# A hybrid decoder layer: the relative bias stored as 23 equal rows a head instead of 128

## The chip, the cores and the metric

The kernel runs on one core of one Trainium2 chip. The metric is the time of one execution on the device in microseconds; the engines are TensorE (PE, with its weight loads as PEld), VectorE (DVE), ScalarE (ACT), GpSimd (POOL) and SyncE (SP), and transfers run on 16 DMA engines.

## The reference

One decoder layer on 256 tokens of width 2048, all in float32: a joint input projection, a Conformer convolution branch and a differential attention branch side by side, an output projection, a cross-attention into 256 memory tokens, a gated FFN with a causal convolution, and a final norm. What matters here is the bias of the differential attention. Each of 8 heads has two score maps, and both get the same bias, which depends only on the distance of query and key:

```python
bias = bias_dist_t[:, jnp.clip(rel, 0, s - 1)].astype(jnp.float32)     # rel = q_pos - k_pos
logits = logits.reshape(b, H_DIFF, 2, Q_BLOCK, s) + bias[None, :, None]
logits = jnp.where(causal[None, None, None], logits, NEG_INF)
```

So within a head the bias matrix has equal diagonals: row q is row 0 shifted by q.

## The kernel before

**Weights.** All matmuls are float32 products made of two parts: a weight chunk of 128 x 1024 (512 KB) is loaded (`raw`), ScalarE rounds it to `hi` (line 157) and VectorE subtracts it to `lo` (line 158), and TensorE multiplies with both. SyncE issues the loads in order (line 146); `raw`, `hi` and `lo` have four buffers each, so a load waits for the subtraction four chunks back, and a rounding for TensorE four chunks back.

**Steps.** The kernel counts its weight chunks, and the other work of the phase is placed at such steps (`STEPS`, `PAIR`). Chunks 0 to 31 are the convolution's gates, 32 to 39 the values of heads 0 to 3, 40 to 71 the queries and keys of four pairs of heads, 8 chunks each. A chunk of a pair is twelve matmuls (lines 209 to 211). TensorE's order is written out by hand; the order on the other engines is made by the framework's planner from modelled times, with hints (`issue_after`) that hang the convolution's taps (line 342, VectorE) on a chunk's subtraction.

**Bias.** At step 43 `bias_rows` multiplies the table of 32 buckets with a one-hot matrix and gets, for each of 8 heads, one row of 384 values: column m is the bias of distance 255 - m, and columns of negative distance hold -1e30, which is the causal mask. ScalarE copies it to `brow` (8 partitions), and GpSimd writes it to a scratch tensor `scr` in memory (line 365). Head by head, `load_bias` reads it back to 128 partitions of 256 columns (line 370), also from GpSimd's queue, with two buffers.

**Heads.** A pair's queries and keys are turned (`turn`, lines 454 and 455, copied by ScalarE at line 457). `scores` multiplies them to logits (lines 466 and 469) in one buffer of PSUM, VectorE adds the bias (line 474), and the softmax and the combination of the two maps follow on VectorE and ScalarE (lines 477 to 485). The stages of a pair come between the next eight chunks: `turn` of its first head at 2 steps behind the pair's end, `scores` of the first and `turn` of the second at 3, `scores` of the second at 4, so for the first pair at steps 50, 51, 51 and 52.

Of the kernel before, what the change touches and what calls it, by code (L numbers as in the profile page):

```python
# [12 lines left out]
F32 = mybir.dt.float32  # L13
# [6 lines left out]
P = 128  # L20
S = 256
NMEM = 256
D = 2048
# [4 lines left out]
NH = 8  # L28
NB = 32
# [10 lines left out]
# columns of the packed per-partition parameters  # L40
# [9 lines left out]
# A step is the number of weight chunks before it: the gates' chunks are 0-31, the values of heads 0-3 take 32-39, the  # L50
# pairs of heads 40-71, the values of heads 4-7 72-79, the memory 80-95, the output projection 96-127, the queries 128-135.
# Behind its chunk, the tensor engine's other work comes at these steps.
# [5 lines left out]
# the same within a pair of heads, from the pair's end  # L58
PAIR = ((2, "turn", 0), (3, "scores", 0), (3, "turn", 1), (4, "scores", 1), (10, "combine", 1), (8, "combine", 0))
# operations of the queue behind each chunk, from that step on  # L60
# [7 lines left out]
def trunk_kernel(ctx, tc, xT_d, memT_d, mem_d, par_d, tab_d, hot_d, gf_d, wa_d, wck_d, wv_d, wqk_d,  # L68
# [19 lines left out]
    # ---- resident data  # L88
# [12 lines left out]
    # the tensor engine's clock rises while it is busy  # L101
# [6 lines left out]
    # ---- work of the other engines that is spread over the weight chunks: behind the rounding (ScalarE) or the  # L108
    # subtraction (VectorE) of a given chunk, and a queue behind the subtractions
# [18 lines left out]
    # ---- work of the tensor engine between the weight chunks, one stage after each  # L128
# [11 lines left out]
    # ---- weight chunks: raw -> (hi, lo), hi + lo == raw exactly  # L140
    sent = []

    def weight(src, name, dst=None, halved=False):
        raw = wp.tile([P, 1024], F32, tag="raw", bufs=4, name="raw_" + name)
        if not halved:
            sent.append(SP.dma_start(out=raw, in_=src).ins)
        hi, lo = dst or (wp.tile([P, 1024], F32R, tag=t, bufs=4, name=f"{t}_{name}") for t in ("hi", "lo"))
        if halved:
            # the first chunk, each half in front of its k-tile of x
            for k, w in enumerate((slice(0, 512), slice(512, 1024))):  # L150
                SP.dma_start(out=raw[:, w], in_=src[:, w])
                SP.dma_start(out=xT[:, k:k + 1, :], in_=xT_d[:, k:k + 1, :])
                A.copy(out=hi[:, w], in_=raw[:, w])
                V.tensor_tensor(out=lo[:, w], in0=raw[:, w], in1=hi[:, w].bitcast(F32), op=ALU.subtract)
            split_x(0)
            return hi, lo
        rounded = A.copy(out=hi, in_=raw)  # L157
        fill(rounded, V.tensor_tensor(out=lo, in0=raw, in1=hi.bitcast(F32), op=ALU.subtract))  # L158
        return hi, lo

    def quarter(name):
        """[hi | lo] of four k-tiles of an activation."""
        return act.tile([P, 4, 2 * S], F32R, tag="act", name=name)
# [4 lines left out]
    def split(dst, src, scale):  # L168
        """dst = [hi | lo] of src * scale (per partition)."""
        hi, lo = dst[:, 0:S], dst[:, S:2 * S]  # L170
        if scale is None:
            A.copy(out=hi, in_=src)
            V.tensor_tensor(out=lo, in0=src, in1=hi.bitcast(F32), op=ALU.subtract)
        else:
            A.activation(out=hi, in_=src, func=AF.Copy, scale=scale)
            V.scalar_tensor_tensor(out=lo, in0=src, scalar=scale, in1=hi.bitcast(F32), op0=ALU.mult,
                                   op1=ALU.subtract)

    def part_b(tiles, c, src, acts, name, first, last, narrow=False):
        """Four k-tiles of two n-tiles, weights stationary: tiles[n] = [w.T @ hi(act) | corrections];  # L180
        narrow: all in the first half."""
        hi, lo = weight(src, f"{name}_{c}")
        for kk in range(4):
            k = 4 * c + kk
            for n in range(2):
                o = kk * S + n * P
                begin, end = first and kk == 0, last and kk == 3
                if narrow:
                    T.matmul(tiles[n][:, 0:S], hi[:, o:o + P], acts(k)[:, 0:S], start=begin, stop=False)
                    T.matmul(tiles[n][:, 0:S], hi[:, o:o + P], acts(k)[:, S:], start=False, stop=False)  # L190
                else:
                    T.matmul(tiles[n], hi[:, o:o + P], acts(k), start=begin, stop=False)  # L192
                T.matmul(tiles[n][:, 0:S] if narrow else tiles[n][:, S:], lo[:, o:o + P], acts(k)[:, 0:S],  # L193
                         start=False, stop=end)
        stage()
# [5 lines left out]
    def part_a(tiles, c, src, acts, name, halved=False):  # L201
        """Two k-tiles: tiles[t] = (tokens of t) x 512 columns, activations stationary."""
        hi, lo = weight(src, f"{name}_{c}", halved=halved)
        for kk in range(2):
            k = 2 * c + kk
            w = slice(kk * 512, kk * 512 + 512)
            for t in range(2):
                ah, al = acts(k)[:, t * P:t * P + P], acts(k)[:, S + t * P:S + t * P + P]
                T.matmul(tiles[t], ah, hi[:, w], start=k == 0, stop=False)  # L209
                T.matmul(tiles[t], ah, lo[:, w], start=False, stop=False)  # L210
                T.matmul(tiles[t], al, hi[:, w], start=False, stop=k == KT - 1)  # L211
        stage()
# [7 lines left out]
    def sum_halves(out, pst, name):  # L220
        """out = main + corrections"""
# [4 lines left out]
    def rsqrt(out, ms, n, eps, shape, name):  # L226
        """out = 1 / sqrt(ms / n + eps), one Newton step behind the table's root."""
# [10 lines left out]
    def sum_all(acc, name):  # L238
        """Sums over the partitions of acc [P, S], on every partition."""
        m = sm_ps("ms_" + name)  # L240
        T.matmul(m[:, 0:S], ones, acc, start=True, stop=True)
        return m[:, 0:S]

    def sum_tok(parts, name):
        """out[p, t] = the sum of parts[:][:, t*128 + p] over their partitions."""
# [6 lines left out]
    def to_row(out, tok, name):  # L252
        """out[p, t*128 + c] = tok[c, t], on every partition p."""
# [8 lines left out]
    # ---- x: split, statistics  # L262
# [7 lines left out]
    def split_x(c):  # L270
        """Two k-tiles."""
# [5 lines left out]
    def total(t):  # L277
        """Sum over the tiles of t [P, 4, S], in place; its first tile is returned."""
# [25 lines left out]
    # ---- convolution module: gate and depthwise convolution  # L304
    gated = {}

    def gate(b):
        """Channel tiles 2b, 2b + 1: [second half | first half] of the projection, tokens on partitions."""
# [42 lines left out]
    # ---- relative bias and lambda  # L351
# [5 lines left out]
    # every row p of a head in memory alike; read back with a pitch shorter by one, row p is shifted by p  # L357
    scr = dr.tile([NH, P, BW], F32, name="scr")

    def bias_rows():  # L360
# [4 lines left out]
        G.dma_start(out=scr, in_=brow.unsqueeze(1).broadcast_to([NH, P, BW]))  # L365

    def load_bias(hd):
        bias = ph.tile([P, S], F32, tag="bias", bufs=2, name=f"bias{hd}")
        base = scr[hd, 0, P - 1:P - 1 + S]
        G.dma_start(out=bias, in_=bass.AP(tensor=base.tensor, offset=base.offset, ap=[[BW - 1, P], [1, S]]))  # L370
# [14 lines left out]
    # ---- differential attention: values  # L385
# [8 lines left out]
    # ---- convolution module: layer norm, silu (into the first half of mix)  # L394
# [39 lines left out]
    # ---- differential attention: heads  # L434
    o4, oss, s_last = {}, {}, [None]

    def pair(b):
        """Queries (scaled) and keys of two heads, tokens on partitions."""
# [20 lines left out]
    def scores(hd):  # L459
        """Both maps of a head, combined, but for the factor r1 of each query."""  # L460
# [10 lines left out]
        for qt in range(2):  # L471
# [10 lines left out]
            # p1 - lam p2, over r1: e1 + e2 * (-lam s1 / s2)  # L482
# [53 lines left out]
    def attend(b, qk):  # L536
        """The stages of a pair of heads, spread over the eight chunks of the next projection."""
# [7 lines left out]
    # ---- memory: split, statistics, keys  # L545
# [16 lines left out]
    def mem_square(t, c):  # L562
        """Sums of squares of a half of the tokens' rows."""
# [8 lines left out]
    def mem_queue(c):  # L572
        """The splits of two quarters, one to each of the next chunks."""
# [63 lines left out]
    # ---- output projection; residual in place; statistics  # L637
# [27 lines left out]
    # ---- cross attention  # L665
# [62 lines left out]
    # ---- its projection; where a part of it can go ahead, heads 0 and 1 first  # L728
# [44 lines left out]
    # ---- gated FFN  # L773
# [9 lines left out]
    def conv_f(i, u, out):  # L783
        """out = causal 3-tap convolution of channel tile i, whose projection u lacks the norm's factor."""
# [7 lines left out]
    for j in range(FT):  # L792
# [23 lines left out]
        if 4 <= j < 12:  # L816
            # residual to token-major
# [9 lines left out]
    # ---- down projection: eight banks, [token tile][column block]  # L827
# [38 lines left out]
    # ---- the last tiles bank after bank; final norm  # L866
# [4 lines left out]
    for t in range(2):  # L871
# [18 lines left out]
        # 1 / sqrt(v) = y0 * (1.5 - 0.5 v y0 y0)  # L890
# [21 lines left out]
# ---- host: layout only  # L912
# [9 lines left out]
def _one_hot():  # L922
    """Column m stands for the distance 255 - m; row NB marks what causality hides."""
# [8 lines left out]
def _cols(v):  # L932
    """(n*128,) -> (128, n)"""
# [3 lines left out]
def _feat(x):  # L937
    """(tokens, D) -> [p, k, token]"""
# [3 lines left out]
def _pair_chunks(w, first, second):  # L942
    """Blocks of two 128-column tiles of w (K, N): [block, chunk of 4 k-tiles, p, k, 256]."""
# [8 lines left out]
def _reorder(w, tiles):  # L952
    """The column tiles of w in that order."""
# [3 lines left out]
def _wide_chunks(w):  # L957
    """(K, n*512) -> [column block, chunk of 2 k-tiles, p, 1024]."""
# [57 lines left out]
```

## Time and profile before

| what | value |
|---|---|
| three runs, median | 1220.07 us (1219.28 to 1221.32) |
| profiled execution: span | 1219.7 us; the page gives no other time for it |
| TensorE busy | 1191.3 us (98%) |
| VectorE busy | 890.7 us (73%) |
| ScalarE busy | 683.2 us (56%) |
| GpSimd busy | 7.5 us (1%) |
| mean granted clock of TensorE | 0.989 |
| DMA | 227.62 MB, mean 187 GB/s |

The span is the time from the first to the last instruction on the core. Busy shares are means over all stages; an engine's wait counts only where something that sets the end is behind it. Times in the rows are microseconds from the span's start. A time to landing is the time from a DMA's issue until all its data have arrived.

### The profile page before, as it was taken

How to read it: one execution, taken by the hardware profiler on the slowest of the kernel's cores; microseconds unless marked ns; L12 is line 12 of the kernel's file. 1: busy time of each engine (PE TensorE's matmuls, PEld its weight loads, DVE VectorE, ACT ScalarE, POOL GpSimd, SP SyncE). 2: the span in 40 equal slices, each digit the busy share in tenths (PEclk: the TensorE clock that was granted, in tenths of full speed). 3: DMA queues.
4: the chain of work that ended last, by engine and by line, in shares of the span. 5: the costliest groups of instructions: out<-in, count | busy, mean ns of one | idle time of the engine just before them, and what ended most of it. 6: DMA issues, size and time to landing. Idle time of an engine off the chain costs nothing.

```text
span 1219.7 us, 16959 instructions
## 1 busy us (share of the span) xinstructions
PE 1191.3 (98%) x6186; PEld 1005.6 (82%) x6186; DVE 890.7 (73%) x1469; ACT 683.2 (56%) x1111; POOL 7.5 (1%) x19
## 2 busy tenths in 40 slices
PE   9999949999999999999999999999999999999997
PEld 7888738888888898888888888888888888888885
DVE  7899759998676778877777777777777756555554
ACT  8644336887755666755555555555555545444443
POOL 0000000000000000000000000000000000000000
PEclk9999979999999999999999999999999999999998
DMA  9656656566565636555665565555555467555541
GB/s 314 207 188 193 151 153 203 182 217 198 160 203 190 188 109 202 181 184 174 214 185 187 190 188 183 186 187 190 185 182 187 172 206 256 190 187 186 189 151 69
DMA packets 64164, 227.62 MB, mean 187 GB/s; under 512 B 7661, under 2 KB 7917, under 8 KB 63952
## 3 DMA queue, kind: packets, MB, share of 16 engines
q1 hardware_dynamic: 62784, 223.85, 56.5%
q0 software_dynamic: 1152, 2.68, 1.5%
q8 instruction: 48, 0.79, 0.2%
q14 instruction: 36, 0.29, 0.1%
q10 hardware_dynamic: 144, 0.01, 0.0%
HBM read 222.83 MB, written 3.67 MB: 186 GB/s over the span
## 4 chain that ended last, share of the span: by engine, by line
PE 93%; DMA 3%; DVE 2%; ACT 1%; issue 0%; SPq 0%; ACTq 0%
PE up L192 27%; PE up L193 14%; PE acc L840 5%; PE acc L841 5%; PE acc L842 5%; PE wo L192 5%; PE wo L193 2%; PE a L210 2%; PE a L211 2%; PE a L209 2%; DMA raw_qk<-in_wqk 2%; PE acc_lg L840 2%; PE acc_lg L841 2%; PE acc_lg L842 2%; PE qk L209 2%; PE qk L211 1%
## 5 line engine op out<-in xcount | busy, mean ns | idle before, releaser
L192 PE MATMUL up<-hf,hi_up 128*128 128x512 f32 x1408 | 497.8, 399 | 0.0
L193 PE MATMUL up<-hf,lo_up 128*128 128x256 f32 x1408 | 395.1, 281 | 0.0
L192 PEld LDWEIGHTS up<-hf,hi_up 128*128 128x128 f32 x1408 | 264.4, 188 | 64.8
L158 DVE TENSOR_TENSOR lo_up<-raw_up,hi_up 128x1024 fp32r<-128x1024 f32 x176 | 215.5, 1225 | 83.2 <-ACT hi_up L157 75.2
L157 ACT CAST hi_up<-raw_up 128x1024 fp32r<-128x1024 f32 x176 | 185.0, 1051 | 153.8 <-PE up L192 112.5
L193 PEld LDWEIGHTS up<-hf,lo_up 128*128 128x128 f32 x1408 | 265.9, 189 | 0.2
L158 DVE TENSOR_TENSOR lo_dn<-raw_dn,hi_dn 128x1024 fp32r<-128x1024 f32 x84 | 102.8, 1225 | 72.5 <-ACT hi_dn L157 72.3
L157 ACT CAST hi_dn<-raw_dn 128x1024 fp32r<-128x1024 f32 x84 | 88.1, 1049 | 64.7 <-PE acc_lg L842 54.0
L841 PE MATMUL acc<-lo_dn,gh 128*128 128x512 f32 x252 | 99.7, 396 | 0.0
L842 PE MATMUL acc<-hi_dn,gl 128*128 128x512 f32 x252 | 99.7, 395 | 0.0
L342 DVE SCALAR_TENSOR_TENSOR y<-ga,par,y 128x249 f32<-128x249 f32 (+17 forms) x240 | 99.0, 463 | 0.0
L840 PE MATMUL acc<-hi_dn,gh 128*128 128x512 f32 x252 | 98.7, 396 | 0.0
L192 PE MATMUL wo<-mix,hi_wo 128*128 128x512 f32 x256 | 89.3, 395 | 0.0
L193 PE MATMUL wo<-mix,lo_wo 128*128 128x256 f32 x256 | 70.6, 278 | 0.0
L223 ACT COPY corr_up<-up 128x256 f32<-128x256 f32 x88 | 32.9, 374 | 66.0 <-PE up L193 66.0
L157 ACT CAST hi_qk<-raw_qk 128x1024 fp32r<-128x1024 f32 x32 | 33.5, 1052 | 51.9 <-DMA raw_qk<-in_wqk 22.6
L224 DVE TENSOR_TENSOR u<-up,corr_up 128x256 f32<-128x256 f32 x88 | 37.1, 421 | 28.7 <-ACT corr_up L223 28.7
L209 PE MATMUL qk<-hi_qk,h 128*128 128x512 f32 x128 | 52.0, 406 | 5.3 <-ACT hi_qk L157 5.3
L840 PEld LDWEIGHTS acc<-hi_dn,gh 128*128 128x128 f32 x252 | 47.4, 188 | 11.5
L192 PEld LDWEIGHTS wo<-mix,hi_wo 128*128 128x128 f32 x256 | 47.9, 188 | 10.8
L842 PEld LDWEIGHTS acc<-hi_dn,gl 128*128 128x128 f32 x252 | 47.4, 188 | 11.4
L841 PEld LDWEIGHTS acc<-lo_dn,gh 128*128 128x128 f32 x252 | 47.4, 188 | 11.3
(300 smaller groups left out, 2007.1 us busy)
## 6 DMA issues: line engine op xcount, KB each, us to landing
raw_up<-in_wup SPq DMA_DIRECT2D x176, 512.0 KB, 3.5
raw_dn<-in_wdn SPq DMA_DIRECT2D x88, 512.0 KB, 4.5
raw_qk<-in_wqk SPq DMA_DIRECT2D x32, 512.0 KB, 4.0
raw_wo<-in_wo SPq DMA_DIRECT2D x32, 512.0 KB, 3.6
raw_a<-in_wa SPq DMA_DIRECT2D x31, 512.0 KB, 4.1
raw_v<-in_wv SPq DMA_DIRECT2D x16, 512.0 KB, 3.6
raw_ck<-in_wck SPq DMA_DIRECT2D x8, 512.0 KB, 3.8
raw_cv<-in_wck SPq DMA_DIRECT2D x8, 512.0 KB, 4.2
```

The costliest lines, as they stand in the source:

```text
L157: rounded = A.copy(out=hi, in_=raw)
L158: fill(rounded, V.tensor_tensor(out=lo, in0=raw, in1=hi.bitcast(F32), op=ALU.subtract))
L192: T.matmul(tiles[n], hi[:, o:o + P], acts(k), start=begin, stop=False)
L193: T.matmul(tiles[n][:, 0:S] if narrow else tiles[n][:, S:], lo[:, o:o + P], acts(k)[:, 0:S], start=False, stop=end)
L209: T.matmul(tiles[t], ah, hi[:, w], start=k == 0, stop=False)
L211: T.matmul(tiles[t], al, hi[:, w], start=False, stop=k == KT - 1)
L223: A.copy(out=c, in_=pst[:, S:])
L224: V.tensor_tensor(out=out, in0=pst[:, 0:S], in1=c, op=ALU.add)
L342: V.scalar_tensor_tensor(out=y[:, j, s:], in0=gated[j][:, 0:S - s], scalar=w, in1=y[:, j, s:], op0=ALU.mult, op1=ALU.add)
L840: T.matmul(acc[t][n], ah, hi, start=f == 0, stop=False)
L841: T.matmul(acc[t][n], ah, lo, start=False, stop=False)
L842: T.matmul(acc[t][n], al, hi, start=False, stop=f == FT - 1)
```

## The change

Two places change; elsewhere the diff only takes comments out. `scr` gets 23 rows of 384 values a head instead of 128, all alike as before. The read-back then goes through memory in two steps: partition p = 16a + b starts at a rows less 16a, and b rows less b, instead of p rows less p. Both ways partition p gets columns 127 - p to 382 - p. The largest row touched is 7 + 15 = 22.

```diff
-    # every row p of a head in memory alike; read back with a pitch shorter by one, row p is shifted by p
-    scr = dr.tile([NH, P, BW], F32, name="scr")
+
+    REP = P // 16 + 15
+    scr = dr.tile([NH, REP, BW], F32, name="scr")
 ...
-        G.dma_start(out=scr, in_=brow.unsqueeze(1).broadcast_to([NH, P, BW]))
+        G.dma_start(out=scr, in_=brow.unsqueeze(1).broadcast_to([NH, REP, BW]))
 ...
-        G.dma_start(out=bias, in_=bass.AP(tensor=base.tensor, offset=base.offset, ap=[[BW - 1, P], [1, S]]))
+        G.dma_start(out=bias, in_=bass.AP(tensor=base.tensor, offset=base.offset,
+                                          ap=[[BW - 16, P // 16], [BW - 1, 16], [1, S]]))
```

## Rows read from the trace of the kernel before

**Rows 1.** The page's 40 slices of the span, busy tenths.

```profile
PE   9999949999999999999999999999999999999997
```

**Rows 2.** Busy time by stretch; behind it clock, DMA share, GB/s.

```profile
122.00:152.20 30.20, 30.20 (x134) 24.16 (x132) 22.88 (x44) 10.03 (x13) 1.10 (x1) 1.00 0.63 152
152.20:178.60 26.40, 10.60 (x38) 7.33 (x37) 12.76 (x23) 7.08 (x8) 1.09 (x2) 0.68 0.62 156
178.60:265.00 86.40, 86.22 (x439) 69.44 (x440) 84.52 (x191) 68.35 (x166) 3.23 (x6) 1.00 0.60 199
...
150.00:155.00 5.00, 2.36 (x13) 1.76 (x11) 0.00 (x0) 0.00 (x0) 0.00 (x0) 0.96 0.50 85
```

**Rows 3.** The chain of waits, 139 to 180 us: start, length, what.

```profile
140.70 28.35 DMA raw_qk<-in_wqk
```

**Rows 4.** ScalarE in order of time, 144 to 175 us: start, length, instruction.

```profile
144.21 0.48 ACT L445 ACTIVATE qk<-qk,rx_tok 128x256 f32<-128x256 f32 x1
156.61 1.04 ACT L157 CAST hi_qk<-raw_qk 128x1024 fp32r<-128x1024 f32 x1 [11.92 <-DMA raw_qk<-in_wqk]
...
171.33 0.58 ACT L457 COPY qkT<-qkT 128x512 f32<-128x512 f32 x1
```

**Rows 5.** TensorE in order of time, from 149 to 180 us.

```profile
149.04 0.39 PE L209 MATMUL qk<-hi_qk,h 128*128 128x512 f32 x1
...
151.76 0.27 PE L454 MATMUL qkT<-ident,qk 128*128 128x128 f32 x1
...
152.09 0.27 PE L455 MATMUL qkT<-ident,qk 128*128 128x128 f32 x1
...
171.96 0.80 PE L466 MATMUL lg<-qkT 64*128 64x128 f32 x4 [9.06 <-ACT qkT L457]
...
178.61 0.49 PE L466 MATMUL lg<-qkT 64*128 64x128 f32 x4 [0.94 <-DVE L L474]
...
179.47 0.50 PE L209 MATMUL qk<-hi_qk,h 128*128 128x512 f32 x1
```

**Rows 6.** DMA issues (120 to 133, 133.6 to 135 us, whole span): KB each, us to landing.

```profile
raw_qk<-in_wqk SPq DMA_DIRECT2D x5, 512.0 KB, 3.6
...
raw_qk<-in_wqk SPq DMA_DIRECT2D x1, 512.0 KB, 21.6
...
xT<-in_xT SPq DMA_DIRECT2D x7, 256.0 KB, 6.6
...
scr<-brow POOLq DMA_DIRECT2D x1, 1536.0 KB, 35.5
bias<-scr POOLq DMA_DIRECT2D x8, 128.0 KB, 3.4
```

**Rows 7.** GpSimd in order of time, 0 to 300 us.

```profile
133.66 1.10 POOL L365 DMA_DIRECT2D scr<-brow  x1 [130.76 <-ACT brow L364]
169.40 1.09 POOL L370 DMA_DIRECT2D bias<-scr  x2 [34.64 <-DMA scr<-brow]
178.76 0.54 POOL L370 DMA_DIRECT2D bias<-scr  x1 [8.26 <-DVE L L474]
```

**Rows 8.** GpSimd's DMA queue, 135-140 and 150-155 us: packets, MB, share.

```profile
q0 software_dynamic: 405, 0.25, 50.8%
...
q0 software_dynamic: 52, 0.24, 40.7%
```

**Rows 9.** VectorE in order of time, 143 to 204 us.

```profile
157.69 1.23 DVE L158 TENSOR_TENSOR lo_qk<-raw_qk,hi_qk 128x1024 fp32r<-128x1024 f32 x1 [12.36 <-ACT hi_qk L157]
...
164.71 1.23 DVE L158 TENSOR_TENSOR lo_qk<-raw_qk,hi_qk 128x1024 fp32r<-128x1024 f32 x1 [5.02 <-ACT hi_qk L157]
...
170.22 1.23 DVE L158 TENSOR_TENSOR lo_qk<-raw_qk,hi_qk 128x1024 fp32r<-128x1024 f32 x1 [3.13 <-ACT hi_qk L157]
...
177.45 1.01 DVE L474 TENSOR_TENSOR L<-lg,bias 128x256 f32<-128x256 f32 x2
...
203.06 1.02 DVE L474 TENSOR_TENSOR L<-lg,bias 128x256 f32<-128x256 f32 x2
```

## The prediction

> **What bounds the kernel now.** I read the page's slices first. TensorE is busy nine tenths or more of every slice but one: the sixth, from 152 to 183 us, reads 4 [rows 1]. So the kernel is bound by TensorE, and a change outside it pays only in that hole. A table of three stretches cuts the hole out: from 122.0 to 152.2 us TensorE is busy throughout, from 152.2 to 178.6 it is busy 10.60 of 26.40 us at a clock of 0.68, and from 178.6 to 265, past the end of the pairs of heads, it is full again [rows 2]. The chain of waits says what the hole is: one piece of 28.35 us, a chunk of query and key weights on its way from memory, released at last at 169.05 [rows 3]; behind it the chain goes on over the rounding and VectorE's work, up to a bias add, to logits on TensorE.
>
> Then the queues. ScalarE rounds each weight chunk and stands idle for 11.92 us in front of the one at 156.61, for the weights' DMA, and again in front of the next; the copy of the turned queries (L457) stands behind those roundings in its queue, at 171.33, and TensorE's logits wait 9.06 us for it [rows 4, 5]. The weights were asked for early enough: a chunk takes 3.6 us to land between 120 and 133 us, the one issued at 134.97 takes 21.6 [rows 6], the one in the chain, issued at 140.70, 28.35. What is new at that moment is the write of the bias rows: GpSimd issues it at 133.66, it takes 35.5 us, and the first read-back starts at 169.40, when it has landed [rows 6, 7]. The software queue holds 51 to 41% of the sixteen engines' time meanwhile, and between 150 and 155 us the DMA share is 0.50 at 85 GB/s: by that I read eight engines full and eight empty, while the weights wait [rows 2, 8]. That is what is late: the half of every weight chunk that lies behind the write on those eight engines.
>
> **The change, part by part.** The write: 8 heads x 128 rows x 1536 B = 1.573 MB become 8 x 23 x 1536 B = 0.283 MB. The software queue moves 0.24 MB in 5 us [rows 8], so 0.048 MB a us; the old write is 32.8 us by that, and 2.7 of its 35.5 us lie around the moving. The new one is 0.283 / 0.048 + 2.7 = 8.6 us, and lands at 133.66 + 8.6 = 142.3. From below the nearest row is a read-back, 128 KB in 3.4 us; from above it is the old write itself, 35.5 us, if the time went by something other than bytes; an x load of 256 KB, nearly the new size, takes 6.6 us [rows 6]. I take 8.6, nearest to that last row.
>
> What is late then? The chunk issued at 134.97 (call it 51, by the kernel's own count of chunks) has its half on the eight engines behind the write. If none of that moves before 142.3 and half a chunk then takes half of 3.6 us, it lands at 144.1, the next two at 145.9 and 147.7. ScalarE wants the first at 144.69, after the four query and key copies [rows 4]; the following ones wait anyway for TensorE to free the rounded chunk four back, at 146.3, 149.0 and 151.8 (a chunk of 2.72 us apart, the last at the end of the matmuls before 151.76 [rows 5]). So no rounding is late.
>
> VectorE next, which has work without a gap in the old trace from 170 on: from the subtraction at 157.69 to the end of the bias add at 178.46 are 20.77 us, less its waits of 5.02 and 3.13, so 12.6 us of work [rows 9]. With the rounding of chunk 51 done at 145.7 it ends at 158.4.
>
> TensorE: between the end of the first turn (152.20) and the logits at 178.61 it does four things. Chunk 51: twelve matmuls, as from 149.04 to 151.76, 2.72 us. The logits of head 0: as from 178.61 to 179.47, 0.86. The turn of head 1: four transposes 0.11 apart from 151.76 on, 0.44, as the one that ended at 152.20. Chunk 52: 2.72. Together 6.74, since the engine no longer idles and its clock stays at 1.00 as in the stretch before [rows 2, 5]. The logits at 178.61 start at 152.20 + 6.74 = 158.94, with VectorE done 0.5 us earlier. The gain is 178.61 - 158.94 = 19.67 us: 15.80 us of idle time and 3.87 of slow matmuls.
>
> From there TensorE has no gap up to the end of the pairs in the old trace, so the whole is shifted and nothing later is given back: the stages behind run on the same prefetch, and the weights' queue is paced by VectorE's subtractions. The cover is thin in one place, VectorE's 0.5 us: each us by which chunk 51 lands after 145.2, that is the write takes over 9.8 us, costs TensorE up to one.
>
> The read-backs keep 128 rows of 1 KB and one issue of 0.54 us each; only the source's steps differ, eight blocks of 16 rows. They were 3.4 us. Bounds: 2.7 us by the write's rate (0.131 / 0.048), and 6.8 if they go on half the engines; I take 3.4 to 6.8 and cost it at nothing, because the bias of heads 0 and 1 is now issued from 142.3 for a use at 157.5, and the third, issued at 178.76, is used at 203.06, 24 us later [rows 7, 9]. Without that cover each would cost its own length. GpSimd has nothing queued behind them but the next read-back.
>
> A rule bears on this. The write, with 8 heads outermost on both sides, fills half the engines (share 0.50 [rows 2]). The Trainium skill, "DMA: Bandwidth & Descriptors", section "Why a DMA increments its semaphore by 16 and not by 1", says the number of engines is the largest up to 16 that divides the outermost size of both sides; the trace agrees for the write, 8 heads and eight engines. By that rule the new read-back, whose source has 8 outermost, drops to eight engines too, which no row here shows; the sum is the same with it, but it speaks for the last rival below.
>
> The sum is made against the profiled execution, of which the page gives the span alone: 1219.7 - 19.7 = 1200.0. The median of the runs, 1220.07, lies 0.4 over that span, and by the same distance the forecast is 1200.4 us.
>
> **The rivals.** *The write shrinks less than its bytes.* A fixed part, or the eight engines clearing late, makes it 10 to 17 us. For it: its first 5 us move 405 packets and only 0.25 MB, so something small goes ahead of the rows [rows 8]. Against it: that stretch moves as many bytes as the later ones. At 14 us chunk 51 is 4.2 us too late: 1204.6; over the whole case 1201 to 1207.
>
> *The planner orders VectorE and ScalarE anew.* Only TensorE's order is written out here; the others follow modelled times, and the write's may be in them. A rounding that slips behind a softmax, or out from behind one, moves one chunk, 2.7 us: 1197.7 to 1203.1. Against it: the bias add stands right behind the logits in the old order, as if the bias were there, so the model hardly saw the write's delay.
>
> *Nothing happens:* the weights are late for another reason, 1220. For it only that the chain names the weights, not the write. Against it: weights and write come free together, at 169.1 and 169.2.
>
> *Read-backs that hold the weights as the write did, on the slower side.* Place: the two read-backs of each pair of heads. The old write held eight engines for 35.5 us and cost 19.67, so prefetch covers 15.8. Two read-backs at 6.8 us each hold 13.6, and cost nothing. Over 7.9 us each they eat into the gain, and it decides at 15.8 + 19.67 / 4 = 20.7 us a pair, 10.4 us a read-back, three times what it is: at 12 us the four pairs lose 4 x 8.2 = 33, and the time is 1233. At 8.5 to 9.5 us they leave a small gain, 1205 to 1213. For it: the two steps and half the engines. Against it: runs of 1 KB are kept.
>
> **How the numbers follow.** My forecast 0.68 (its own range 1198.8 to 1202.0), the write 0.14, the planner 0.11, read-backs that eat a part 0.03, read-backs slower than before 0.02, nothing 0.02. The range 1198.0 to 1205.0 holds the first, three quarters of the second and nearly all of the third, about 0.88 on paper; I keep it, because the write's length rests on one rate. About 0.2% is what a measurement of this kernel can tell from no change: faster 0.96, same 0.02, slower 0.02.
>
> **What would show it.** The profile after should have the write at 6 to 10 us to landing; weight chunks of that stretch under 10 us; no rounding that idles for a DMA; a sixth slice at 9 and a clock of 1.00 throughout it; the second logits near 159 and everything behind them about 19.7 us earlier; read-backs of 3 to 7 us, landed long before their bias adds. I am wrong if the write stays over 10 us, if VectorE ends its bias add after 159, or if the order of the roundings differs from before.

## The result, and the profile after

The changed kernel takes 1200.78 us (1200.46 to 1202.04), the kernel before 1220.09 (1219.28 to 1221.32): a ratio of 0.984, 95% interval 0.9827 to 0.9854, faster by 19.3 us. The instructions stand in the same order on every engine in both; only the shapes of the bias transfers differ.

The sixth slice is full now (the page's slices, busy tenths; the kernel after). The last slice, 7 before and 6 now, is the kernel's tail; the prediction passed over it when it wrote "every slice but one".

```profile
PE   9999999999999999999999999999999999999996
```

The same by stretches (length, then busy time and instructions of TensorE, its weight loads, VectorE, ScalarE and GpSimd; clock, DMA share, GB/s), which answer to [rows 2]:

```profile
122.00:152.20 30.20, 30.20 (x135) 24.23 (x134) 29.08 (x54) 13.92 (x17) 1.88 (x3) 1.00 0.73 200
152.20:159.00 6.80, 6.80 (x40) 4.79 (x39) 6.75 (x15) 2.70 (x4) 0.59 (x1) 1.00 0.65 205
159.00:246.00 87.00, 86.83 (x439) 70.13 (x438) 84.91 (x192) 69.78 (x169) 2.94 (x5) 1.00 0.62 197
```

From 122 to 159 us TensorE has no idle time and its clock no dip. The DMA issues (KB each, us to landing; the weight chunk is chunk 51, issued at 133.54) answer to [rows 6]:

```profile
raw_qk<-in_wqk SPq DMA_DIRECT2D x1, 512.0 KB, 8.0
...
bias<-scr POOLq DMA_DIRECT2D x8, 128.0 KB, 4.3
scr<-brow POOLq DMA_DIRECT2D x1, 276.0 KB, 7.4
```

ScalarE in order of time. The rounding of chunk 51 stands right behind the query and key copies and waits for nothing, and the turned queries follow at 151.48, where [rows 4] have them at 171.33:

```profile
142.77 0.48 ACT L447 ACTIVATE qk<-qk,rx_tok 128x256 f32<-128x256 f32 x1
143.13 1.06 ACT L157 CAST hi_qk<-raw_qk 128x1024 fp32r<-128x1024 f32 x1
...
151.48 0.57 ACT L459 COPY qkT<-qkT 128x512 f32<-128x512 f32 x1
```

VectorE from that chunk's subtraction to the bias add, for [rows 9]:

```profile
144.22 1.23 DVE L158 TENSOR_TENSOR lo_qk<-raw_qk,hi_qk 128x1024 fp32r<-128x1024 f32 x1 [0.33 <-ACT hi_qk L157]
...
156.31 1.02 DVE L476 TENSOR_TENSOR L<-lg,bias 128x256 f32<-128x256 f32 x2
```

TensorE from the end of the first turn over chunk 51 to the first logits, then the second turn, chunk 52 and the second logits, for [rows 5]; there is no wait in brackets anywhere:

```profile
150.65 0.27 PE L457 MATMUL qkT<-ident,qk 128*128 128x128 f32 x1
150.68 0.47 PE L209 MATMUL qk<-hi_qk,h 128*128 128x512 f32 x1
...
153.60 0.49 PE L468 MATMUL lg<-qkT 64*128 64x128 f32 x4
...
154.87 0.48 PE L209 MATMUL qk<-hi_qk,h 128*128 128x512 f32 x1
...
157.81 0.49 PE L468 MATMUL lg<-qkT 64*128 64x128 f32 x4
```

GpSimd, for [rows 7]:

```profile
132.23 0.68 POOL L366 DMA_DIRECT2D scr<-brow  x1 [129.31 <-ACT brow L365]
139.88 1.20 POOL L371 DMA_DIRECT2D bias<-scr  x2 [6.97 <-DMA scr<-brow]
157.62 0.59 POOL L371 DMA_DIRECT2D bias<-scr  x1 [16.54 <-DVE L L476]
```

Where the time went can be read off the rows. From the write's issue to the second logits are 178.61 - 133.66 = 44.95 us before and 157.81 - 132.23 = 25.58 after: 19.37 us. From there to the end of the span are 1041.1 us in both. The write itself is issued 1.43 us earlier in this execution, which the change has no part in: between 10 and 20 us the granted clock was 0.83 in the profiled run of before, a mean over the two levels, and 1.00 in that of after. So the spans, 1219.7 and 1198.9, differ by 20.8, and the medians by 19.3.

The third read-back waits for the first bias add, so the time from the write's issue to its issue (the write-to-third-read time below) measures the hole in any of these kernels without that start: 178.76 - 133.66 = 45.10 before, 157.62 - 132.23 = 25.39 after.

### The profile page after: what moved, and what is told of

The parts are those of the page before. It is cut to its first block, busy times and chain, and to the rows that moved or that the text cites. A ratio compares the mean times of both kernels' runs of the same rounds, so it can differ in the third digit from the quotient of the medians.

```text
span 1198.9 us, 16959 instructions
## 1 busy us (share of the span) xinstructions
PE 1186.8 (99%) x6186; PEld 1003.0 (84%) x6186; DVE 891.0 (74%) x1469; ACT 683.0 (57%) x1111; POOL 7.5 (1%) x19
## 4 chain that ended last, share of the span: by engine, by line
PE 98%; ACT 1%; DMA 0%; DVE 0%; SPq 0%; issue 0%; ACTq 0%
PE up L192 28%; PE up L193 14%; PE acc L843 5%; PE acc L844 5%; PE acc L842 5%; PE wo L192 5%; PE qk L209 2%; PE wo L193 2%; PE qk L211 2%; PE qk L210 2%; PE a L210 2%; PE a L211 2%; PE a L209 2%; PE acc_lg L843 2%; PE acc_lg L844 2%; PE acc_lg L842 2%
## 5 line engine op out<-in xcount | busy, mean ns | idle before, releaser
L209 PE MATMUL a<-hi_a,h 128*128 128x512 f32 x128 | 51.0, 398 | 0.5 <-ACT hi_a L157 0.5
```

## The experiments

My theory: the write keeps the weight chunks back on the engines that it fills, and how long it does so goes by its bytes. Its rivals: the form of the read-back, a bias that comes too late for the scores, and causes that the rows do not set.

**One half of the change: two-step read-back, 128 rows.**

```diff
-    REP = P // 16 + 15
+    REP = P
```

> 128 rows a head are written as before, and read back with the two steps of the changed kernel (one half of the change). Theory (the write holds eight DMA engines and so the weights): the write takes 35 us again and the time is that of before, 1220. Rival (the form of the read-back makes the gain): 1201.

Measured: 1219.77 us, ratio to before 1.0003 (0.9994 to 1.0012). The DMA issues of this run:

```profile
scr<-brow POOLq DMA_DIRECT2D x1, 1536.0 KB, 34.7
bias<-scr POOLq DMA_DIRECT2D x8, 128.0 KB, 3.9
```

The read-back's form alone changes nothing; all of the gain is in the 23 rows.

**Half the rows.**

```diff
-    REP = P // 16 + 15
+    REP = 64
```

> The changed kernel with 64 rows a head instead of 23. Theory: the write goes by its bytes, 64 x 0.256 us + 2.7 = 19.1 us to landing; each us over 9.8 costs up to one us of TensorE, so up to 9.3 us: at most 1210, and at least half of that, 1205. Rival (a loss in proportion to the rows, with no cover): 19.3 x 41 / 105 = 7.5 us, 1208. Rival (the write has a length that rows don't set): 1201 or 1220.

Measured: 1211.23 us (1209.07 to 1213.08), ratio 0.9924 (0.9909 to 0.9939); the write lands after 18.2 us. That is a little over my 1210, and the total alone does not tell my range from the rival's 1208; the waits in the trace do. They show both terms of the sum and one that I had left out (the rounding of chunk 51; the second logits; the stretch behind them):

```profile
151.14 1.04 ACT L157 CAST hi_qk<-raw_qk 128x1024 fp32r<-128x1024 f32 x1 [7.91 <-DMA raw_qk<-in_wqk]
```

```profile
164.80 0.49 PE L468 MATMUL lg<-qkT 64*128 64x128 f32 x4 [3.24 <-DVE L L476]
```

```profile
165.00:170.00 5.00, 5.00 (x20) 3.77 (x19) 5.00 (x14) 1.86 (x8) 1.09 (x2) 0.66 0.47 126
```

The chunk is rounded 8.0 us later than after the change, VectorE's 12.4 us of work follow at once, and TensorE waits for the bias add as the prediction's thin place has it: the logits come 164.80 - 157.81 = 6.99 us later. Behind the wait, in which TensorE was idle for 3.24 us, the granted clock is 0.66 for 5 us, and the third to the fifth read-back are 27.17 us apart instead of 25.93, another 1.2 us. Together that is 8.2 of the 8.4 us by which its span is longer than that of after. This was the fastest of its four executions (1209.07); the others, 1210.96 to 1213.08, had mean granted clocks of 0.992 to 0.996 instead of 0.997, but where they lost it no trace here shows.

**The write 46 us earlier, 128 rows.** The block that makes the bias moves ahead of the gates, and its step from 43 to 26:

```diff
-STEPS = dict(x_square=(2, 4, 7, 8), x_add=(5, 7, 9), stats=9, gated=(12, 22, 24, 36), bias=43, lam=46,
+STEPS = dict(x_square=(2, 4, 7, 8), x_add=(5, 7, 9), stats=9, gated=(12, 22, 24, 36), bias=26, lam=46,
...
+    at(STEPS["bias"], bias_rows)
+    for b in range(CT // 2):
+        at(STEPS["gated"][b], gated_T, b, gate(b))
...
-    at(STEPS["bias"], bias_rows)
```

> The kernel before, with 128 rows, but the bias rows are made and written at step 26 instead of 43, some 46 us earlier; the read-backs of heads 0 and 1 then land long before the scores. Theory (the write starves the weight chunks that are loaded beside it): the hole moves to 90 to 130 us and costs 15 to 20 us there, 1216 to 1222. Rival (the scores wait for a bias that comes too late): no hole, 1201.

Measured: 1217.91 us, ratio 0.9982 (0.9973 to 0.9991). The bias is read back at 120, over 50 us before its use, and the hole has moved to the write's new place (five-us stretches of this run, then its GpSimd):

```profile
105.00:110.00 5.00, 1.50 (x7) 0.92 (x5) 0.00 (x0) 0.00 (x0) 0.00 (x0) 0.86 0.53 113
110.00:115.00 5.00, 1.48 (x3) 0.88 (x4) 1.97 (x4) 1.42 (x2) 0.00 (x0) 0.50 0.52 86
```

```profile
85.51 1.10 POOL L359 DMA_DIRECT2D scr<-brow  x1 [82.63 <-ACT brow L358]
120.05 1.09 POOL L371 DMA_DIRECT2D bias<-scr  x2 [33.44 <-DMA scr<-brow]
```

TensorE is idle there for 3.5 of every 5 us with nobody waiting for a bias. So it is by the weights that the write costs time, 17.1 us over the changed kernel here; VectorE's order differs in places in this one, so the 2.1 us less than before are not to be read closely.

**All 128 rows, written from 16 partitions.** The product makes each head's row twice, and each of 16 partitions writes 64 copies:

```diff
...
-        G.dma_start(out=scr, in_=brow.unsqueeze(1).broadcast_to([NH, P, BW]))
+        G.dma_start(out=scr.rearrange("h (n r) w -> (h n) r w", n=2),
+                    in_=brow.unsqueeze(1).broadcast_to([2 * NH, P // 2, BW]))
...
```

> The kernel before with all its 128 rows, written from 16 partitions (each head's row twice, 64 rows from each) instead of 8, so that 16 lies outermost on both sides. Theory (eight engines, each at its own rate): all sixteen work at it, the write takes 16.4 + 2.7 = 19 us, and the loss is between 5 and 11 us: 1206 to 1212. Rival (the write's rate is set elsewhere, in memory or in the queue): 35 us still, 1220.

Measured: 1209.71 us, ratio 0.9915 (0.9898 to 0.9933), and 18.9 us to landing. The stretch from 140 to 145 us, and the DMA queues in it:

```profile
140.00:145.00 5.00, 5.00 (x24) 4.13 (x23) 4.65 (x9) 2.63 (x5) 0.00 (x0) 1.00 0.99 101
```

```profile
q0 software_dynamic: 110, 0.51, 99.2%
```

With 16 partitions the share is 0.99 where it was 0.50 with 8: the number of engines follows the outermost size. And there is no row of the weights' queue: with all sixteen engines full, no weight packet passes in these 5 us, nor in any of the 12 us from 136 to 148, in which 258 of the write's do.

**All 128 rows, written from 128 partitions.** The same once more, with each head's row on 16 partitions and 8 copies from each:

```diff
...
-        G.dma_start(out=scr, in_=brow.unsqueeze(1).broadcast_to([NH, P, BW]))
+        G.dma_start(out=scr.rearrange("h (n r) w -> (h n) r w", n=16),
+                    in_=brow.unsqueeze(1).broadcast_to([P, P // 16, BW]))
...
```

> The kernel before with all its 128 rows, written from 128 partitions (each head's row on 16 partitions, 8 rows from each) instead of 8. Theory A (an engine takes some 0.7 us for each 4 KB of this write however many partitions it reads from, and sixteen work): 19 us, as with 16 partitions, and 1208 to 1212. Theory B (an engine is slow because it reads one partition over and over): the write runs at the rate of a weight load, 1.5 MB in 8 to 10 us, and the time is 1201 to 1203, with all 128 rows.

Measured: 1201.13 us, ratio 0.9847 (0.9831 to 0.9864), as fast as the changed kernel with all its 1.5 MB. The write, and the queues between 134 and 138 us, where the weights' queue has no row:

```profile
scr<-brow POOLq DMA_DIRECT2D x1, 1536.0 KB, 7.9
```

```profile
q0 software_dynamic: 285, 1.31, 101.6%
```

Theory A is out, and B's forecast holds: the engines move 0.51 MB in 99.2% of 16 x 5 us, 6.4 KB a us each, in the write from 16 partitions, and 1.31 MB in 101.6% of 16 x 4 us, 20.1 KB a us each, in the write from 128. B's reason is not shown by that. No trace says which partitions an engine reads, and the rate may as well go by how many the write reads in all (some 0.05, 0.10 and 0.33 MB a us from 8, 16 and 128 partitions); a write from 16 partitions that do not lie side by side might tell, and was not run. This write shuts the weights out too while it lasts, but it is over before chunk 51 is wanted. Bytes alone were never what made the write long.

**The write from ScalarE's hardware queue**, 128 rows from 8 partitions:

```diff
-        G.dma_start(out=scr, in_=brow.unsqueeze(1).broadcast_to([NH, P, BW]))
+        A.dma_start(out=scr, in_=brow.unsqueeze(1).broadcast_to([NH, P, BW]))
```

> The kernel before, with its 128 rows from 8 partitions, but the write is issued from ScalarE's hardware queue instead of GpSimd's software queue. Theory (an engine that reads one partition over and over is slow, and what shares it waits, whichever queue): 30 to 36 us to landing and 1216 to 1222. Rival (the software queue is what keeps the weights back): the write is as long, but the weights get their turns, 1201 to 1208.

Measured: 1219.36 us, ratio 0.9991 (0.9981 to 1.0). ScalarE's queue, q10, between 140 and 145 us:

```profile
q10 hardware_dynamic: 162, 0.25, 47.3%
```

The write moves at the same 0.25 MB in 5 us and the read-backs start 35.5 us behind it, at 167.98, so its slowness is not the software queue's. The weights do fare better, chunk 51 is rounded at 152.60 instead of 156.61, but not because this queue lets them pass where GpSimd's does not. Both writes shut them out at first: with loads under way, their queue has no packet from 146 to 148 us here and none from 142 to 144 in the kernel before. Later both share. The queues from 150 to 155 us, here and then, for [rows 8], the weights' in the kernel before:

```profile
q1 hardware_dynamic: 161, 0.56, 28.0%
q10 hardware_dynamic: 147, 0.23, 23.9%
```

```profile
q1 hardware_dynamic: 54, 0.18, 9.2%
```

With the 52 packets and 40.7% of [rows 8] the shares add up to 49.9% before, and to 51.9% here: by that I read the same eight engines for both, with write and weights taking turns on them, about one packet for one. ScalarE's packets hold 1.6 KB and GpSimd's 4.6, so the weights get three times the turns here. It does not help the time, because a later rounding then waits 8.41 us for its weights, up to 169.02.

**The read-back with 16 outermost.**

```diff
-                                          ap=[[BW - 16, P // 16], [BW - 1, 16], [1, S]]))
+                                          ap=[[BW - 8, P // 8], [BW - 1, 8], [1, S]]))
```

> The changed kernel with the read-back stepped as 8 a + b (16 blocks of 8 rows, the same 23 rows in memory), so that 16 lies outermost in its source instead of 8. Theory: the read-back is off the path, so the time stays at 1201 within 0.2%; if the outermost size sets the number of engines, the read-backs' 4.3 us to landing go back to the 3.4 of before. Rival (the read-backs on eight engines cost the weights a part of the gain): 1197 to 1199.

Measured: 1200.83 us, ratio 0.9842 (0.9828 to 0.9857).

```profile
bias<-scr POOLq DMA_DIRECT2D x8, 128.0 KB, 3.2
```

The read-backs go from 4.3 to 3.2 us, and the time does not move: they were off the path.

**16 outermost on both transfers**, 24 rows a head from 16 partitions, beside the read-back just shown:

```diff
-    REP = P // 16 + 15
+    REP = 24
...
+        G.dma_start(out=scr.rearrange("h (n r) w -> (h n) r w", n=2),
+                    in_=brow.unsqueeze(1).broadcast_to([2 * NH, REP // 2, BW]))
...
```

> The changed kernel with 16 outermost on both transfers: the bias rows are written from 16 partitions (24 rows a head, 12 from each) and read back as 8 a + b. Theory (TensorE has no gap left beside the write): the write goes from 7.4 us to 4 to 5 and the time stays at 1201 within 0.2%. Rival (a part of the stall is left at 23 rows on eight engines): 1197 to 1199.

Measured: 1200.27 us (1200.20 to 1204.03), ratio 0.9844 (0.9827 to 0.9861). The write lands after 5.0 us instead of 7.4, and the write-to-third-read time is 25.41 us against 25.39: nothing was left to win there. This was the version that might have beaten both; it equals the changed one.

**Four read-backs for each.**

```diff
+    spare = [dr.tile([P, S], F32, name=f"spare{i}") for i in range(3 * NH)]
...
-        G.dma_start(out=bias, in_=bass.AP(tensor=base.tensor, offset=base.offset,
+        for to in (bias, *(spare[3 * hd + i] for i in range(3))):
+            G.dma_start(out=to, in_=bass.AP(tensor=base.tensor, offset=base.offset,
...
```

> The changed kernel with each head's read-back issued four times from the same source, the copies going to scratch memory that nobody reads: eight such DMAs for a pair of heads, 1 MB instead of 0.26. Theory (a read-back leaves room for the weights, and prefetch covers some 10 us of blocking): at most 2 us, 1201 to 1203. Rival (a read-back holds its eight engines as the write did): eight at 2.7 to 4.3 us hold 22 to 34 us, 12 to 24 us over the cover in each pair from the second on, 1240 or more.

Measured: 1200.92 us, ratio 0.9845 (0.983 to 0.9859). The planner issued all 24 extra ones in a row, from 140.84 to 158.9, a harder case than the one I had described:

```profile
150.00:155.00 5.00, 5.00 (x31) 3.76 (x30) 4.95 (x12) 2.58 (x3) 4.06 (x8) 1.00 1.03 393
```

All engines are full at 393 GB/s and TensorE still does not idle. A read-back does not hold the weights as the write did.

## Why the prediction was right

Point by point, by its own steps:

- **The cause** (the weights kept back on the eight engines that the write fills): shown. Taking the rows away gives the gain, moving the write moves the hole (128 rows early), and the form of the read-back gives nothing. One part of the picture is off: the half chunks do not stand behind the write until it ends. In the kernel before, the rounding of chunk 52 starts at 163.63 and that of chunk 51 at 156.61, 5.5 and 12.5 us before the write lands, because from some 150 us on the weights take turns with it. Only chunk 53, the one in the chain, comes free with the write, as the prediction had it for the weights. The sum is not touched by that, since at 23 rows the write is over after 7.4 us.

```profile
163.63 1.04 ACT L157 CAST hi_qk<-raw_qk 128x1024 fp32r<-128x1024 f32 x1 [5.97 <-DMA raw_qk<-in_wqk]
```

- **The write at 8.6 us**: 7.4 measured, inside its 6 to 10. Its rate was right, but the 2.7 us around the moving were too many.
- **Chunk 51 on time**: it landed 8.0 us after its issue and its rounding waited for nothing.
- **VectorE 0.5 us ahead of the second logits**: its bias add ended at 157.33, 0.48 before them.
- **TensorE's 6.74 us**: 157.81 - 150.76 = 7.05 measured (the first turn's end as the prediction took it, 0.11 behind the start of its last transpose). The term that was small is the chunk: 2.92 and 2.94 us from its first matmul to the logits, where I had 2.72 from a chunk among chunks. So the gain was 19.37 by the trace where I had 19.67.
- **Nothing given back later**: 1041.1 us to the end in both traces.
- **From the span to the median**: two small errors met. The profiled execution of after took 1200.73 us with a span of 1198.9, so 1.8 us lie around a span, and not the 0.4 that I read off as the distance to the median; and the profiled execution of before had lost 1.43 us to the clock at its start, so by those 1.8 us it lay about as much above its median. That the forecast, 1200.4, came out only 0.4 under the median is luck of these two; what the rows carry is the gain.
- **The read-backs hidden, at 3.4 to 6.8 us**: 4.3 at the median, 6.2 at most. The Trainium skill, "DMA: Bandwidth & Descriptors", section "Why a DMA increments its semaphore by 16 and not by 1", has the engines follow the outermost size; the shares of 0.50 and 0.99 with 8 and 16 partitions agree for the write. For the read-back 3.2 us with 16 outermost against 4.3 with 8 fit it, and with 16 the third read-back takes 62.2% of the engines from 159.1 to 159.9 us, more than eight of them.
- **The rivals**: the planner kept every order. The write's length was no trouble at 23 rows; with 64 its loss went the way of the formula and a slow clock came on top.

One reason behind a term does not hold in general. I scaled the write by its bytes, which is right only among writes from the same eight partitions: the same 1.573 MB take 35.5 us from 8, 18.9 from 16 and 7.9 from 128. Why a write from few partitions is slow, and why the weights get no packet beside it at first and take turns with it later, stays open.

## What to carry to other kernels

A transfer that nobody waits for can still set the end, by the engines that it fills: when prefetched loads are late, look at which other DMA was issued just before, and whether the DMA share stands at a plain fraction such as 0.50. A broadcast from a few partitions is dear for what it holds up; writing less of it and spreading its source over all partitions bought the same 19 us here. Price such a hole by replaying each engine's work at full speed from its start, and take the durations from places with the same neighbours.

## What the hardware showed that I had not expected

- One DMA engine moved 6.4 KB a us in a write from 16 partitions and 20.1 in the same write from 128, in packets of the same 4.6 KB.
- While a write filled all engines, the weights' queue got no packet: none in 12 us beside the write from 16 partitions, none in 4 us beside that from 128. In the kernel before, 16 us and more after the write's issue, the two took turns on eight engines, 54 weight packets beside 52, and with the smaller packets of ScalarE's queue 161 beside 147.
- 24 extra read-backs in 18 us, at a DMA share of up to 1.03, cost the kernel nothing.
